# One-hot on Pool for 5120 columns, and half-block transfers, in a cross-entropy backward kernel

## The chip, the cores and the metric

One core of one Trainium2 chip. The metric is the device time of one launch in microseconds (us); lower is better. Unless a run is called slow, the times are of its fast runs. Each experiment ran beside runs of the kernel before on the same chip.

The problem is bound by memory traffic from the outset: 268.4 MB of float32 logits come in and 268.4 MB of result go out. All that a schedule can do is keep the 16 DMA engines busy from the first byte to the last.

## The reference, cut to what matters

```python
logits: (8, 1024, 8192) float32      labels: (8, 1024) int32
logits_max  = np.max(logits, axis=-1, keepdims=True)
exp_logits  = np.exp(logits - logits_max)
softmax     = exp_logits / np.sum(exp_logits, axis=-1, keepdims=True)
one_hot[batch_idx, seq_idx, labels] = 1.0
return (softmax - one_hot).astype(np.float32)
```

## The kernel before

The 8192 rows of 8192 columns are cut into 32 blocks of 256 rows. A partition holds two neighbouring rows of a block (j = 0, 1), so a block is 128 runs of 64 KB in HBM. Three block buffers in SBUF turn round. In what follows a "row" is one j, that is 128 rows of the problem, 4.19 MB; a block is two of them.

The mode strings have a letter for each block: r, each row is its own transfer (128 runs of 32 KB); w, the whole block is one transfer (128 runs of 64 KB); h, which the kernel before has in its table but doesn't use, two transfers, of the even and of the odd partitions (64 runs of 64 KB each).

```python
LOADS  = "rrrrrwwwwwwwwwwwwwwwwwwwwwrrrrrr"
STORES = "rrrrrrrrrrrrrrrrrrrrrrrrrrrrrrrr"
PIECES = {
    "r": [(every, slice(j, j + 1)) for j in range(G)],
    "h": [(slice(i, P, 2), rows) for i in range(2)],
    "w": [(every, rows)],
}
def load(b):            # issued by SP; waits for those stores of block b - 3 that touch the piece
    ...
def store(t):           # issued by ACT; a piece goes out when its last row is finished
    ...
for t in range(T):      # T = 64
    w = ACT  activation(Exp, bias=-max, accum_out=s)          # in place, 8192 columns
    w_sum = DVE reciprocal(r, s)
    if t + 1 < T:
        if (t + 1) % G == 0: load((t + 1) // G)
        w_max = row_max(t + 1)                                # DVE tensor_reduce
    if t > 0: store(t - 1)
    ACT  activation(Copy, scale=r)                            # 8192 columns
    DVE  scalar_tensor_tensor(x, iota == label, x - that)     # iota: int16 in PSUM
    ...                                                       # cut: last row in two parts
store(T - 1)
```

## Time and profile before

| | before |
|---|---|
| median | 1247.6 us |
| span of the profiled run | 1245.6 us |
| DVE busy | 1115.9 us |
| ACT busy | 919.0 us |
| DMA packets | 15,460 |
| 64 KB load packets, mean | 2421 ns |

The median is that of the timed runs, the next four rows are from the page of the profile, the last is from the packet records of the trace: one record for each contiguous run that a DMA engine moved, with its start and its duration. **Dry time** is how far the number of packets in flight fell short of 16 (one for each engine), integrated from the first data packet to the last and divided by 16. **Excess** is the time by which packets took longer than 2418 ns (64 KB) or 1213 ns (32 KB), which are their medians in this kernel, summed and divided by 16. The kernel before has 1.7 us of dry time and 2.3 us of excess: its engines are full, and its packets are as short as they get.

### The profile page before, as it was taken

The page shows a single profiled execution, that of the slowest core. Times are in us where ns is not written, and L with a number is a line of the kernel's source. Part 1 is how long each engine was busy: PE and PEld are TensorE (multiplying, and loading weights), DVE is VectorE, ACT ScalarE, POOL GpSimd, SP SyncE. Part 2 cuts the span into 40 slices and gives each one's busy share as a digit, 9 for nine tenths or more (in the row PEclk, how much of TensorE's full clock was granted, in tenths as well). Part 3 has the DMA queues.
Part 4 walks back from the last instruction along what each step waited for, and adds up shares of the span by engine and source line. Part 5 has one row for each costly group of instructions (what it writes and reads, how often), then busy time and mean ns, then how long its engine had stood idle before and what let it go on. Part 6 is the DMA issues. An engine that isn't in the chain of part 4 may idle for free.

```text
span 1245.6 us, 592 instructions
## 1 busy us (share of the span) xinstructions
PE 0.4 (0%) x2; PEld 0.3 (0%) x2; DVE 1115.9 (90%) x196; ACT 919.0 (74%) x194; POOL 7.4 (1%) x7
## 2 busy tenths in 40 slices
PE   0000000000000000000000000000000000000000
PEld 0000000000000000000000000000000000000000
DVE  4999997888988889888898888988889999999893
ACT  3888886678767787767867678777777788887772
POOL 2000000000000000000000000000000000000000
DMA  9999999999999999999999999999999999999998
GB/s 398 427 428 432 437 436 441 436 431 425 426 438 448 432 416 440 431 436 438 426 446 437 418 434 432 435 437 442 425 427 438 430 429 437 435 431 431 436 434 388
DMA packets 15460, 536.98 MB, mean 431 GB/s; under 512 B 1728, under 2 KB 1728, under 8 KB 1760
## 3 DMA queue, kind: packets, MB, share of 16 engines
q1 hardware_dynamic: 6240, 268.50, 50.0%
q10 hardware_dynamic: 9216, 268.44, 49.9%
q14 instruction: 4, 0.03, 0.0%
HBM read 268.50 MB, written 268.44 MB: 431 GB/s over the span
## 4 chain that ended last, share of the span: by engine, by line
DMA 60%; DVE 37%; ACT 1%; DVEq 0%; issue 0%; ACTq 0%; SPq 0%
DMA X<-in_logits_dram 32%; DMA out_dram<-X 28%; DVE m L68 19%; DVE X L68 18%; ACT X L68 1%; DVEq L56 0%; DVE r L68 0%; ACTq L68 0%; SPq L223 0%; SPq L56 0%
## 5 line engine op out<-in xcount | busy, mean ns | idle before, releaser
L68 DVE TENSOR_REDUCE m<-X 128x1 f32<-128x8192 f32 x64 | 555.2, 8674 | 108.5 <-DMA X<-in_logits_dram 108.5
L68 ACT ACTIVATE X<-X,m 128x8192 f32<-128x8192 f32 x64 | 455.8, 7122 | 190.2 <-DVE m L68 190.2
L68 DVE SCALAR_TENSOR_TENSOR X<-iota,lab,X 128x8192 f32<-128x8192 int16 (+1 forms) x65 | 559.6, 8611 | 4.1 <-ACT X L68 4.1
L68 ACT ACTIVATE X<-X,r 128x8192 f32<-128x8192 f32 (+1 forms) x65 | 456.0, 7016 | 115.4 <-DVE r L68 115.4
L68 ACT ACTIVATION_READ_ACCUMULATOR X<-X,m 128x1 f32 x64 | 12.0, 187 | 0.0
L68 DVE RECIPROCAL r<-s 128x1 f32<-128x1 f32 x64 | 9.8, 153 | 1.7 <-ACT X L68 1.7
L68 POOL IOTA X<- 128x8192 int16 x1 | 6.9, 6943 | 0.0
L68 DVE TENSOR_SCALAR iota<-X 128x4096 int32<-128x4096 int32 x1 | 4.4, 4428 | 0.1
L68 ACT ACT_TABLE_LOAD x1 | 1.3, 1283 | 0.9 <-SPq L56 0.9
L68 DVE COPY lab<-iota 128x64 f32<-128x64 f32 x1 | 0.2, 225 | 0.5 <-PE iota L68 0.5
L68 PE MATMUL iota<-ident,lab_f 32*128 32x32 f32 x2 | 0.4, 299 | 22.4 <-DVE lab_f L68 22.4
L68 DVE CAST lab_f<-lab_raw 32x256 f32<-32x256 int32 x1 | 0.4, 363 | 0.0
L68 PEld LDWEIGHTS iota<-ident,lab_f 32*128 32x128 f32 x2 | 0.3, 193 | 22.4 <-DVE lab_f L68 22.4
L68 POOL TENSOR_SCALAR_AFFINE_SELECT ident<-ident 32x32 f32<-32x32 f32 x1 | 0.2, 203 | 0.1
L68 POOL MEMSET ident<- 32x32 f32 x1 | 0.1, 115 | 0.5 <-SPq L56 0.5
L212 POOL MEMSET const-bfloat16-1.0<- 128x1 bf16 x1 | 0.1, 106 | 0.0
L212 POOL MEMSET const-uint8-127<- 128x1 uint8 x1 | 0.1, 106 | 0.0
L212 POOL MEMSET const-float32-0.0<- 128x1 f32 x1 | 0.1, 103 | 0.2 <-issue 0.2
L212 POOL MEMSET const-float32-1.0<- 128x1 f32 x1 | 0.1, 103 | 0.0
## 6 DMA issues: line engine op xcount, KB each, us to landing
out_dram<-X ACTq DMA_DIRECT2D x64, 4096.0 KB, 30.9
X<-in_logits_dram SPq DMA_DIRECT2D x22, 4096.0 KB, 27.5
X<-in_logits_dram SPq DMA_DIRECT2D x21, 33.2
lab_raw<-in_labels_dram SPq DMA_DIRECT2D x1, 64.0 KB, 12.3
```

Source lines behind the costliest of these rows:

```text
L68: instruction = getattr(engine, method)(**operands)
L212: nc = _bacc.Bacc("TRN2", target_bir_lowering=False, num_devices=1)
```

## The change

The intent: free ACT and shorten a row by letting idle Pool make most of the one-hot mask; and move 64 KB runs in both directions, in halves, so that the load of a slot's even partitions can start when the store of these has landed.

```diff
-LOADS = "rrrrrwwwwwwwwwwwwwwwwwwwwwrrrrrr"
-STORES = "rrrrrrrrrrrrrrrrrrrrrrrrrrrrrrrr"
+HOT = 5120
+CHUNK = 1280
+LOADS = "rrhhhhhhhhhhhhhhhhhhhhhhhhhhhrrr"
+STORES = "rrrrhhhhhhhhhhhhhhhhhhhhhhrrrrrr"
 ...            (labels, identity and iota are now made before the first row, in an X slot)
+        def row_hot(t):        # waits for w_used[t - 2], the reader of the same mask buffer
+            for k in range(0, HOT, CHUNK):
+                gpsimd.tensor_scalar(out=hot[:, t % 2, k : k + CHUNK], in0=chunk_iota,
+                                     scalar1=label(t) - k, op0=Alu.is_equal)     # int16 -> uint8
 ...
+        def row_finish(t, w_exp):
+            vector.reciprocal(r, s)
+            scalar.activation(x[:, rest], func=Copy, scale=r)                    # 3072 columns
+            vector.scalar_tensor_tensor(x[:, hot_cols], x[:, hot_cols] * r - hot[:, t % 2, :])
+            vector.scalar_tensor_tensor(x[:, rest], iota == label, x - that)     # as before
 ...
+        for b in range(B):
+            load(b); row_hot(2b); row_hot(2b + 1); row_max(2b); row_max(2b + 1)
+            store(2b - 1); row_exp(2b); row_finish(2b)
+            row_exp(2b + 1); store(2b); row_finish(2b + 1)
```

(Shortened: each call also carries its semaphores.)

More of the change, by code (lines that the diff above doesn't have):

```diff
@@ L36 @@
     B = T // G
+    REST = V - HOT
     lab_bp = labels.rearrange("a b -> (a b)").rearrange("(b q) -> b q", q=G * P)
@@ L45 @@
     X = const.tile([P, SLOTS, G, V], fp32)
-    lab_raw = const.tile([B, G * P], labels.dtype)
-    lab_f = const.tile([B, G, P], fp32)
-    ident = const.tile([B, B], fp32)
-    lab = const.tile([P, G, B], fp32)
+    lab = {k: const.tile([P, G, B], fp32, name=f"lab{k}") for k in range(0, HOT, CHUNK)}
     m, s, r = (const.tile([P, T], fp32, name=n) for n in ("m", "s", "r"))
-    iota = psum.tile([P, V], i16)
+    chunk_iota = const.tile([P, CHUNK], i16)
+    hot = const.tile([P, 2, HOT], mybir.dt.uint8)
+    iota = psum.tile([P, REST], i16)
     lab_ps = iota[:].bitcast(fp32)[:, :T].rearrange("p (j b) -> p j b", j=G)
-    with tc.tile_critical():
+    early = X[:, SLOTS - 1, 0, :]
+    lab_raw = early.bitcast(labels.dtype)[:B, : G * P]
+    at = G * P * mybir.dt.size(labels.dtype) // 4
+    lab_f = early[:B, at : at + G * P].rearrange("b (p j) -> b j p", j=G)
+    ident = early[:B, at + G * P : at + G * P + B]
+    made = X[:, SLOTS - 1, G - 1, :].bitcast(i16)[:, :REST]
+    with tc.tile_critical(no_gpsimd_drain=True):
         sem = tc.alloc_semaphore
-        got = [[sem(f"got{i}{q}") for q in range(2)] for i in range(SLOTS)]
-        put = [[sem(f"put{i}{q}") for q in range(2)] for i in range(SLOTS)]
+        got = [[sem(f"got{i}{j}") for j in range(G)] for i in range(SLOTS)]
+        put = [[sem(f"put{i}{j}") for j in range(G)] for i in range(SLOTS)]
         lab_got, dve, act, pe, pool = (sem(n) for n in ("lab_got", "dve", "act", "pe", "pool"))
@@ L74, in run @@
             return counter, count[counter.name]
+        w_raw = run(nc.scalar, [], lab_got, "dma_start", out=lab_raw, in_=lab_bp)
+        w = run(nc.gpsimd, [], pool, "memset", ap=ident, constant=0.0)
+        w_ident = run(
+            nc.gpsimd, [w], pool, "affine_select",
+            out=ident, in_=ident, compare_op=Alu.not_equal, fill=1.0,
+            base=0, pattern=[[-1, B]], channel_multiplier=1,
+        )
+        w_made = run(
+            nc.gpsimd, [], pool, "iota",
+            out=made, pattern=[[1, REST]], base=HOT, channel_multiplier=0,
+        )
+        w_chunk = run(
+            nc.gpsimd, [], pool, "iota",
+            out=chunk_iota[:], pattern=[[1, CHUNK]], base=0, channel_multiplier=0,
+        )
+        step = mybir.dt.size(labels.dtype) // 4
+        lab32 = lab_raw.bitcast(i32).rearrange("b (p j s) -> b j p s", j=G, s=step)
+        w_lab = run(nc.vector, [w_raw], dve, "tensor_copy", out=lab_f, in_=lab32[:, :, :, 0])
+        for j in range(G):
+            w = run(
+                nc.tensor, [w_ident, w_lab], pe, "transpose",
+                out=lab_ps[:, j, :], in_=lab_f[:, j, :], identity=ident,
+            )
+        for k in lab:
+            w_turned = run(
+                nc.vector, [w], dve, "tensor_scalar",
+                out=lab[k][:], in0=lab_ps, scalar1=float(k), scalar2=None, op0=Alu.subtract,
+            )
+        w_iota = run(
+            nc.vector, [w_turned, w_made], dve, "tensor_scalar",
+            out=iota[:].bitcast(i32), in0=made.bitcast(i32), scalar1=0, scalar2=None, op0=Alu.bitwise_or,
+        )
         every, rows = slice(0, P), slice(0, G)
@@ L87, in meets @@
             return all(x & y for x, y in zip(*sets))
-        loaded, stored, finished = {}, {}, []
-        last_made = []
-        def load(b, behind_first=lambda: None):
+        loaded, stored, finished = {}, {}, {}
+        def load(b):
             loaded[b] = []
-            before = stored.get(b - SLOTS, last_made if b == SLOTS - 1 else [])
+            before = stored.get(b - SLOTS, [((every, rows), w_iota)] if b == SLOTS - 1 else [])
             for q, piece in enumerate(PIECES[LOADS[b]]):
@@ L103, in load @@
                 loaded[b].append((piece, w))
-                if q == 0:
-                    behind_first()
         def store(t):
@@ L122, in row, with label @@
             return X[:, t // G % SLOTS, t % G, :]
+        def label(t, less=0):
+            return lab[less][:, t % G, t // G : t // G + 1]
+        w_max, w_sum, w_hot, w_used = {}, {}, {}, {}
+        def row_hot(t):
+            first = [w_chunk, w_turned] if t == 0 else [w_used[t - 2]] if t > 1 else []
+            for k in range(0, HOT, CHUNK):
+                w = run(
+                    nc.gpsimd, first if k == 0 else [], pool, "tensor_scalar",
+                    out=hot[:, t % 2, k : k + CHUNK], in0=chunk_iota[:],
+                    scalar1=label(t, k), scalar2=None, op0=Alu.is_equal,
+                )
+            w_hot[t] = w
         def row_max(t):
@@ L126, in row_max @@
             arrived = [w for piece, w in loaded[b] if meets(piece, (every, slice(j, j + 1)))]
-            return run(
+            w_max[t] = run(
                 nc.vector, arrived, dve, "tensor_reduce",
@@ L130, in row_max @@
             )
-        w_raw = []
-        load(0, lambda: w_raw.append(run(nc.sync, [], lab_got, "dma_start", out=lab_raw[:], in_=lab_bp)))
-        w_max = row_max(0)
-        w = run(nc.gpsimd, [], pool, "memset", ap=ident[:], constant=0.0)
-        w_ident = run(
-            nc.gpsimd, [w], pool, "affine_select",
-            out=ident[:], in_=ident[:], compare_op=Alu.not_equal, fill=1.0,
-            base=0, pattern=[[-1, B]], channel_multiplier=1,
-        )
-        made = X[:, SLOTS - 1, G - 1, :].bitcast(i16)[:, :V]
@@ L144 @@
-        w_made = run(
-            nc.gpsimd, [], pool, "iota", out=made, pattern=[[1, V]], base=0, channel_multiplier=0
-        )
-        step = mybir.dt.size(labels.dtype) // 4
-        lab32 = lab_raw[:].bitcast(i32).rearrange("b (p j s) -> b j p s", j=G, s=step)
-        w_lab = run(nc.vector, w_raw, dve, "tensor_copy", out=lab_f[:], in_=lab32[:, :, :, 0])
-        for j in range(G):
-            w = run(
-                nc.tensor, [w_ident, w_lab], pe, "transpose",
-                out=lab_ps[:, j, :], in_=lab_f[:, j, :], identity=ident[:],
-            )
@@ L155, with row_exp @@
-        w_turned = run(nc.vector, [w], dve, "tensor_copy", out=lab[:], in_=lab_ps)
-        w_iota = run(
-            nc.vector, [w_turned, w_made], dve, "tensor_scalar",
-            out=iota[:].bitcast(i32), in0=made.bitcast(i32), scalar1=0, scalar2=None, op0=Alu.bitwise_or,
-        )
-        last_made.append(((every, slice(G - 1, G)), w_iota))
-        for t in range(T):
+        def row_exp(t):
             x = row(t)
-            label = lab[:, t % G, t // G : t // G + 1]
-            w = run(
-                nc.scalar, [w_max], act, "activation",
+            return run(
+                nc.scalar, [w_max[t]], act, "activation",
@@ L168 @@
                 out=x, in_=x, func=Act.Exp, bias=m[:, t : t + 1], scale=1.0, accum_out=s[:, t : t + 1],
             )
-            w_sum = run(nc.vector, [w], dve, "reciprocal", out=r[:, t : t + 1], in_=s[:, t : t + 1])
-            if t + 1 < T:
-                if (t + 1) % G == 0:
-                    load((t + 1) // G)
-                w_max = row_max(t + 1)
+        def row_finish(t, w_exp):
+            x = row(t)
+            hot_cols, rest = slice(0, HOT), slice(HOT, V)
+            w_sum = run(nc.vector, [w_exp], dve, "reciprocal", out=r[:, t : t + 1], in_=s[:, t : t + 1])
+            w_rest = run(
+                nc.scalar, [w_sum], act, "activation",
+                out=x[:, rest], in_=x[:, rest], func=Act.Copy, bias=0.0, scale=r[:, t : t + 1],
+            )
+            w_used[t] = run(
+                nc.vector, [w_hot[t], w_sum], dve, "scalar_tensor_tensor",
+                out=x[:, hot_cols], in0=x[:, hot_cols], scalar=r[:, t : t + 1], in1=hot[:, t % 2, :],
+                op0=Alu.mult, op1=Alu.subtract,
+            )
+            finished[t] = run(
+                nc.vector, [w_rest], dve, "scalar_tensor_tensor",
+                out=x[:, rest], in0=iota[:], scalar=label(t), in1=x[:, rest],
+                op0=Alu.is_equal, op1=Alu.subtract, reverse1=True,
+            )
@@ L175 @@
+        for b in range(B):
+            load(b)
+            row_hot(b * G)
+            row_hot(b * G + 1)
+            t = b * G
+            row_max(t)
+            row_max(t + 1)
             if t > 0:
                 store(t - 1)
-            n = 1 if t + 1 < T else 2
-            cols = [slice(i * V // n, (i + 1) * V // n) for i in range(n)]
-            scaled = [
-                run(
-                    nc.scalar, [w_sum], act, "activation",
-                    out=x[:, c], in_=x[:, c], func=Act.Copy, bias=0.0, scale=r[:, t : t + 1],
-                )
-                for c in cols
-            ]
@@ L187 @@
-            for c, w in zip(cols, scaled):
-                w = run(
-                    nc.vector, [w], dve, "scalar_tensor_tensor",
-                    out=x[:, c], in0=iota[:, c], scalar=label, in1=x[:, c],
-                    op0=Alu.is_equal, op1=Alu.subtract, reverse1=True,
-                )
-            finished.append(w)
+            w = row_exp(t)
+            row_finish(t, w)
+            w = row_exp(t + 1)
+            store(t)
+            row_finish(t + 1, w)
         store(T - 1)
@@ L196 @@
             for _, w in stored[b]:
-                nc.scalar.wait_ge(*w)
+                nc.sync.wait_ge(*w)
 _INS = ['logits', 'labels']
```

## The prediction

> **What bounds the kernel now.** I read the page first: engine shares, the slices, the queues.
>
> ```profile
> PE 0.4 (0%) x2; PEld 0.3 (0%) x2; DVE 1115.9 (90%) x196; ACT 919.0 (74%) x194; POOL 7.4 (1%) x7
> ...
> DMA  9999999999999999999999999999999999999998
> ...
> DMA packets 15460, 536.98 MB, mean 431 GB/s; under 512 B 1728, under 2 KB 1728, under 8 KB 1760
> ...
> q1 hardware_dynamic: 6240, 268.50, 50.0%
> q10 hardware_dynamic: 9216, 268.44, 49.9%
> ```
>
> The reader is to see that DVE is 90% busy and yet not the bound: the DMA row is 9 in all slices but one. 268.4 MB in and 268.4 MB out are the least the problem allows, and no part of the change moves fewer bytes. Then the chain of waits in order of time, for what a block costs:
>
> ```profile
> 906.93 27.44 DMA out_dram<-X
> 934.39 33.30 DMA X<-in_logits_dram
> 967.71 8.69 DVE m L68
> 976.40 8.66 DVE X L68
> ```
>
> From one such store to the next it is some 77.4 us, for two blocks of 256 rows: 38.7 us a block. A block is 8.39 MB in and 8.39 MB out; 16.78 MB in 38.7 us is 433.5 GB/s. So the chain, though it passes through 17.4 us of DVE, goes at the pace of the queues: its transfers stretch to fill the time. The windows of 20 us say the same, DMA share 0.95 to 1.07 from 20 us to 1240 us. The packet records of the trace settle it: 16 packets (one for each DMA engine) are in flight at nearly every instant of the 1242 us from the first data packet to the last. There is next to no DMA idle time to recover; before and after those 1242 us lie 3.5 us of span, and the timed median is 2.0 us above the span (1247.63 against 1245.6).
>
> The durations for the working come from the groups, with shapes kept apart:
>
> ```profile
> L68 DVE TENSOR_REDUCE m<-X 128x1 f32<-128x8192 f32 x64 | 555.2, 8674 | 108.5 <-DMA X<-in_logits_dram 108.5
> L68 DVE SCALAR_TENSOR_TENSOR X<-iota,lab,X 128x8192 f32<-128x8192 int16 x63 | 550.7, 8742 | 0.0
> L68 ACT ACTIVATE X<-X,m 128x8192 f32<-128x8192 f32 x64 | 455.8, 7122 | 190.2 <-DVE m L68 190.2
> ...
> L68 DVE SCALAR_TENSOR_TENSOR X<-iota,lab,X 128x4096 f32<-128x4096 int16 x2 | 8.9, 4480 | 4.1 <-ACT X L68 4.1
> L68 ACT ACTIVATE X<-X,r 128x4096 f32<-128x4096 f32 x2 | 7.3, 3700 | 1.8 <-DVE r L68 1.8
> L68 POOL IOTA X<- 128x8192 int16 x1 | 6.9, 6943 | 0.0
> ```
>
> The reader is to see two sizes of the same operation, which give a slope and a fixed part, and that DVE waits 108.5 us in all for loads: compute waits for DMA, not the reverse.
>
> **What the Trainium skill says.** (1) "DMA: Bandwidth & Descriptors", section "Where 436 GB/s comes from": 16 ports of 32 B at 850 MHz give 435.2 GB/s. The trace agrees: 433.5 in the middle. At that rate 536.98 MB take 1234 us, so no schedule of these bytes can be 2% faster (under 1222.7). (2) Same page, "Queues, rings and completion order": each DMA engine takes turns between queues packet by packet. So 64 KB load packets against 32 KB store packets favour loads, and equal packets share evenly; the trace's 8 MB loads (33.3 us) beside 4 MB stores (27.4 us) fit. (3) "SBUF — State Buffer", "Who interferes with whom": a DVE instruction with two SBUF inputs and a GpSimd instruction that reads SBUF exclude each other, and the later one waits for the whole of the earlier. The kernel before cannot show it: its iota lies in PSUM, and Pool is silent after 8 us. (4) "GPSIMD Engine Reference", section 7: a compare body took 2.03 cycles an element, 1.03 when unrolled. No row before has a Pool compare; IOTA's 6943 ns for 8192 is 1.02 cycles at 1.2 GHz.
>
> **The change, part by part.**
>
> Transfers. The packet records give 1213 ns for 32 KB and 2418 ns for 64 KB: 8 ns saved where one large packet replaces two. Before: 11,008 small (8192 stores, 2816 loads) and 2,688 large. After: loads are 5 blocks by rows (1,280 small) and 27 in halves (3,456 large); stores are 10 by rows (2,560 small) and 22 in halves (2,816 large). So 3,584 pairs merge: 3,584 x 8 ns / 16 engines = **1.8 us less**. Half transfers also double the semaphore packets of a block move, 9 ns each: nothing.
>
> ACT. The scaling falls from 8192 to 3072 columns. 8192 take 7.12 us and 4096 take 3.70: 0.835 ns a column and 0.28 fixed, so 2.85 us. ACT loses 64 x 4.27 = 273 us of busy time. It was not the bound, so this is worth nothing directly.
>
> DVE. The last step becomes 5120 and 3072 columns. Slope (8.74 - 4.48)/4096 = 1.04 ns, fixed 0.22: 5.55 + 3.41 = 8.96 us, and consecutive ones overlap by 0.1. The busy time stays near 64 x (8.67 + 8.96 + 0.15) = 1138 us.
>
> Schedule of one block (two rows) after its load, with starts on DVE: two maxima 0 to 17.2; exp of the first row meanwhile on ACT (8.7 to 16.0); reciprocal 17.3; compared part 17.5 to 23.0; rest 23.0 to 26.3 (ACT's Copy ends at 20.4). ACT's second exp runs 20.4 to 27.7, so DVE idles 1.4 us. Second reciprocal 27.8, compared part 28.0 to 33.5, rest to 36.8. So **36.8 us a block** against 38.7 of DMA: DMA still sets the pace, by 1.9 us. Before, DVE needed 2 x 17.44 = 34.9 us a block, so the new order is tighter.
>
> Pool. Four compares of 1280 a row. At 1.03 to 2.03 cycles an element, 1.2 GHz and an assumed 0.1 us of start, one is 1.2 to 2.3 us and a row 4.8 to 9.1 us (an estimate from the GPSIMD page). A row's compares may begin only when the buffer's reader two rows earlier has ended, that is at 23.0 in the block, and the second compared part wants to start at 28.0: 5.0 us later. With fast compares Pool is just done; with slow ones DVE waits for the compare in flight, at most 2.3 us. The other row's compares (from 33.5) fall beside the maxima and harm nobody. I put the block at 37.5.
>
> Start and end. Label work leaves the path behind the first maximum and runs before the first row lands (13.4 us): neutral. A loss: a half load needs both row stores of its slot. Walking the start at 433 GB/s, row stores go out near 42, 51, 79, 88 us; the queues run dry for perhaps 1 us near 79, when the load of block 3 waits for the store of row 1 to land, and for up to 2.5 us near 196, when block 4 (first stored in halves) finishes as both queues empty. At the end, row stores again: with four rows outstanding at the last load, the last two come 19 and 28 us later, just in time; up to 3 us may be lost. I take **2 us of new DMA idle time** in all, out of a possible 0 to 6.
>
> Sum: 1247.6 - 1.8 + 2.0 = 1247.8; the kernel's strings of modes look chosen by trial, which makes me lean to less idle time: **1246.5 us**.
>
> **Rivals.** (a) Compute takes over: the block exceeds 38.7 us. First row after 13.4 us, then 32 blocks, then about 15 us for the last store: 28.4 + 32 x C. C = 38.0 gives 1244, so it begins to bind there; C = 38.8 (the worst single wait) gives 1270; C = 40 gives 1308. For it: DVE at 90%, the two SBUF inputs, Pool's compares starting right ahead of the contended step. Against it: only one compare should be in the way, and short chunks look meant for that. If Pool held the ports for all four compares in a row, C would near 41 and the time 1340. (b) Transfers over 64 alternate partitions go slower than over 128: nothing in the profile before speaks of such a transfer, since it has none; at 5% less the time would be 1305. Even and odd partitions spread over the same places, so I give it little. (c) The relief of ACT and earlier loads shorten the time: against it, the DMA row is full everywhere, so at most a microsecond or two at the ends. (d) The new waits at the changes of mode cost more than I walked through, say 8 us: 1254.
>
> **Range and chances.** Floor: no new idle and a little better packing, 1243. Likely: 1245 to 1250. (d) and mild (a) reach 1262. So 1242 to 1260 should hold 8 times in 10. Faster by 2% is barred by bytes over rate: 0.01. Slower by 2% (over 1272.6) needs rival (a) in its bad form or (b): 0.08. Within: 0.91.
>
> **What would show it.** Right: DMA slices still 9 throughout, near 433 GB/s; fewer packets (about 12,200 in all); ACT near 646 us, DVE near 1140 us plus contention, Pool 310 to 580 us; the chain still mostly DMA; 64 KB packets still 2418 ns. Wrong: DMA slices of 8 and DVE at 9 to 10 throughout with the compared step well over 5.55 us would mean rival (a); long packets at full DMA share, rival (b); single low slices near 80 and 196 us or at the end, rival (d). The weakest steps are the Pool compare's duration and who yields when it meets DVE.

## The result

The changed kernel takes **1267.9 us** (median of 4 runs, 1265.5 to 1268.4) against 1247.6 us (1247.3 to 1248.1). The ratio is 1.0158, 95% interval 1.0141 to 1.0176: slower by 1.6%, within 2%, but outside the range I had given. (A ratio here is the mean time of one kernel's fast runs over that of the other's fast runs of the same rounds, so not quite the ratio of the medians.)

The page of the changed kernel: engine shares, the DMA row and the rate in 40 slices, the packet count, and three groups (busy time and mean of one | idle time before, and for what).

```profile
PE 0.4 (0%) x2; PEld 0.3 (0%) x2; DVE 1186.3 (94%) x262; ACT 642.5 (51%) x193; POOL 1076.4 (85%) x264
...
DMA  9999998999999999999999999999999999999996
GB/s 400 415 423 430 434 429 359 431 429 432 440 431 423 440 440 442 431 431 428 431 429 429 429 431 434 431 442 436 434 432 431 429 432 424 430 431 437 433 417 284
DMA packets 12216, 537.01 MB, mean 425 GB/s; under 512 B 2064, under 2 KB 2064, under 8 KB 2096
...
L80 POOL TENSOR_SCALAR hot<-chunk_iota,lab 128x1280 uint8<-128x1280 int16 x256 | 1072.1, 4196 | 154.7 <-DVE X L80 153.3
...
L80 DVE TENSOR_REDUCE m<-X 128x1 f32<-128x8192 f32 x64 | 552.9, 8679 | 23.2 <-DMA X<-in_logits_dram 23.2
L80 DVE SCALAR_TENSOR_TENSOR X<-X,r,hot 128x5120 f32<-128x5120 f32 x64 | 411.0, 6422 | 2.3
```

Read it against the lines of before in the prediction. ACT fell by 276 us, as worked out, and it bought nothing. DVE rose by 70 us: its 5120-column step takes 6.42 us on average. Pool's compare takes 4.2 us for 1280 columns. And the DMA row, full before, has two holes: slice 7 (190 to 221 us) at 359 GB/s and the last slice at 284.

The time line of one block in the middle (start, duration, engine, what; in brackets the idle time before and its releaser) shows the meeting of DVE and Pool:

```profile
573.89 5.55 DVE L80 SCALAR_TENSOR_TENSOR X<-X,r,hot 128x5120 f32<-128x5120 f32 x1
...
579.54 32.82 POOL L80 TENSOR_SCALAR hot<-chunk_iota,lab 128x1280 uint8<-128x1280 int16 x8 [6.45 <-DVE X L80]
...
584.09 7.37 DVE L80 SCALAR_TENSOR_TENSOR X<-X,r,hot 128x5120 f32<-128x5120 f32 x1
591.38 3.40 DVE L80 SCALAR_TENSOR_TENSOR X<-iota,lab,X 128x3072 f32<-128x3072 int16 x1
```

The first row's step takes 5.55 us while Pool stands still. It frees Pool's buffer, Pool starts eight compares, and the second row's step, 4.5 us later, takes 7.37 us: 1.82 us more. If eight compares share the 32.82 us with one DVE step of 5.55 us, a compare takes 3.4 us, and the second one would end 6.8 us after 579.54, at 586.4; 584.09 + 1.82 is 585.9. The two agree to half a microsecond: the step waits for about the rest of the compare in flight, then goes ahead of the next one.

The end of the changed kernel, the four last stores that ACT issues:

```profile
1202.33 0.34 ACTq L80 DMA_DIRECT2D out_dram<-X  x1
...
1214.34 0.34 ACTq L80 DMA_DIRECT2D out_dram<-X  x1
...
1240.51 0.34 ACTq L80 DMA_DIRECT2D out_dram<-X  x1
...
1250.70 0.34 ACTq L80 DMA_DIRECT2D out_dram<-X  x1
```

All loads have landed by then. 26 us pass between the second and third of these stores; a row takes some 10 us to move alone (4.19 MB at 433 GB/s), so the queue runs out.

**Where the 17 us went, by the packet records.** From the first data packet to the last the changed kernel takes 1259.3 us against 1242.1. Dry time rose from 1.7 to 13.6 us (3.9 us from 170 to 215 us, 8.8 us from 1220 us on). Excess rose from 2.3 to 8.6 us, nearly all of it in 64 KB loads, whose mean is 2453 ns against 2421. Merged packets gave back 1.8 us. 11.9 + 6.3 - 1.8 = 16.4 us; packets overlap a little less, which is the rest. This is book-keeping: idle engines and long packets must add up to the time, and it names no cause. The question is whether the compute made the transfers late, or the transfers themselves are worse.

### The profile page after: what moved, and what is told of

Its sections match the earlier page's. It is cut to its first block, busy times and chain, and to the rows that moved or that the text cites. A ratio compares the mean times of both kernels' runs of the same rounds, so it can differ in the third digit from the quotient of the medians.

```text
span 1263.7 us, 1041 instructions
## 1 busy us (share of the span) xinstructions
PE 0.4 (0%) x2; PEld 0.3 (0%) x2; DVE 1186.3 (94%) x262; ACT 642.5 (51%) x193; POOL 1076.4 (85%) x264
## 2 busy tenths in 40 slices
DMA packets 12216, 537.01 MB, mean 425 GB/s; under 512 B 2064, under 2 KB 2064, under 8 KB 2096
## 4 chain that ended last, share of the span: by engine, by line
DMA 39%; DVE 28%; ACT 12%; POOL 10%; issue 10%; ACTq 0%; SPq 0%; DVEq 0%
DMA out_dram<-X 22%; DMA X<-in_logits_dram 17%; DVE m L80 15%; DVE X L80 12%; ACT X L80 12%; POOL hot L80 10%; DVE r L80 0%; ACTq L80 0%; SPq L80 0%; DVEq L79 0%; SPq L261 0%; SPq L68 0%
## 5 line engine op out<-in xcount | busy, mean ns | idle before, releaser
L80 POOL TENSOR_SCALAR hot<-chunk_iota,lab 128x1280 uint8<-128x1280 int16 x256 | 1072.1, 4196 | 154.7 <-DVE X L80 153.3
L80 DVE TENSOR_REDUCE m<-X 128x1 f32<-128x8192 f32 x64 | 552.9, 8679 | 23.2 <-DMA X<-in_logits_dram 23.2
L80 DVE SCALAR_TENSOR_TENSOR X<-X,r,hot 128x5120 f32<-128x5120 f32 x64 | 411.0, 6422 | 2.3
L80 DVE SCALAR_TENSOR_TENSOR X<-iota,lab,X 128x3072 f32<-128x3072 int16 x64 | 218.1, 3408 | 0.0
L80 ACT ACTIVATE X<-X,r 128x3072 f32<-128x3072 f32 x64 | 182.8, 2857 | 56.8 <-DVE r L80 56.8
L80 POOL IOTA X<- 128x3072 int16 x1 | 2.7, 2677 | 0.0
```

The lines of the kernel that those rows point to most:

```text
L80: instruction = getattr(engine, method)(**operands)
```

## The experiments

Theory A: the compute. DVE's step meets Pool's compares, a block takes 38.0 to 38.2 us in place of 36.3, and so the queues go dry at both ends. Theory B: the order, both maxima ahead of the first finish, which makes the last stores late. Theory C: the transfers in halves.

### Strings and compute taken apart (e1, e2)

```diff
 e1: the changed kernel
-LOADS = "rrhhhhhhhhhhhhhhhhhhhhhhhhhhhrrr"        +LOADS = "rrrrrwwwwwwwwwwwwwwwwwwwwwrrrrrr"
-STORES = "rrrrhhhhhhhhhhhhhhhhhhhhhhrrrrrr"       +STORES = "rrrrrrrrrrrrrrrrrrrrrrrrrrrrrrrr"
 e2: the kernel before, with the opposite edit
```

> The changed kernel with the two mode strings of the kernel before (row and whole-block loads, row stores); the compute is the changed one. Theory A (compute has become the pace at both ends: DVE's compared step meets Pool's compares, 38.0 to 38.2 us a block instead of 36.3): the block stays at 38.0 to 38.2 us, the queues still run dry near the end, time 1260 to 1268 us. Theory C (the half transfers cost it: the dry spell near 190 us and the slower 64 KB load packets): both go away, time 1248 to 1256 us.

> The kernel before with the mode strings of the changed kernel; the compute is the old one. Theory A: no loss, 1245 to 1250 us, 64 KB packets at 2418 ns. Theory C: 1255 to 1265 us, with 64 KB load packets averaging above 2440 ns and a dry spell of some us where the stores change to halves.

e1: **1249.0 us**, ratio to before 1.0003 (0.9988 to 1.0018), correct. e2: **1281.4 us**, ratio 1.0264 (1.0244 to 1.0284). Theory C wins outright, and for e2 by more than it asked: by the ratios the strings cost 2.6% (33 us) with the old compute and 1.6% (19 us) with the new. The whole new compute, contention and order included, costs under 1 us. The page of e1:

```profile
PE 0.4 (0%) x2; PEld 0.3 (0%) x2; DVE 1183.2 (95%) x262; ACT 642.3 (51%) x193; POOL 1153.2 (92%) x264
...
DMA  9999999999999999999999999999999999999998
...
L80 DVE TENSOR_REDUCE m<-X 128x1 f32<-128x8192 f32 x64 | 552.6, 8672 | 10.4 <-DMA X<-in_logits_dram 10.4
L80 DVE SCALAR_TENSOR_TENSOR X<-X,r,hot 128x5120 f32<-128x5120 f32 x64 | 409.7, 6401 | 2.3
```

The step takes as long as ever (6.40 us), and the DMA row is full again. The telling figure is in the first group: the maxima wait 10.4 us in all for loads, 23.2 us in the changed kernel. (On the first two rows it is 3.7 us in e1 and 6.0 us in the changed kernel; the rest comes later.) At 38.1 us a block, compute has 0.6 us a block to spare against the 38.7 us of transfers, so one reading is that compute can't catch up on late loads, and the last stores are late for it. e3, below, speaks against this as the whole cause. The order alone (Theory B) costs nothing either: e1 has the same order and only 2.4 us of dry time.

### Pool's compares taken out, and the ports taken apart (e3, e4, e5, e12)

```diff
 e3: the changed kernel
         def row_hot(t):
+            if t > 1:
+                w_hot[t] = w_hot[t - 2]
+                return
 e4: the changed kernel; fake is a uint8 tile in PSUM, set to 0 once
-                ... in1=hot[:, t % 2, :],
+                ... in1=fake[:],
 e5: e3 with the old LOADS and STORES
 e12: the changed kernel
-CHUNK = 1280
+CHUNK = 640
```

> The changed kernel, but Pool compares only for rows 0 and 1 and later rows use those masks (wrong result on purpose). Everything else stays. Theory A: the 5120-column step falls from a mean of 6.42 to 5.55 us, the block to 36.3 us, the DMA idle time near the end shrinks, time 1248 to 1256 us. Theory C: block shorter too, but time 1260 or more, since the transfers are the same. Theory B (the order: both maxima ahead of the first finish, so that the last stores come late): time stays above 1258 us with a dry spell of 6 us or more at the end.

> The changed kernel with Pool's compares as they are, but DVE's 5120-column step reads its mask from a constant tile in PSUM (wrong result on purpose), so that it has one SBUF input. Theory A, in the form that the two exclude each other over SBUF inputs: the step takes 5.55 us though Pool is as busy, Pool's compares take 3.4 to 3.5 us each and never stand still for the step, and the time equals that of the run with Pool silent within 2 us. If Pool's work slows DVE in another way: the step stays near 6.4 us and the time near 1266 us.

> The changed kernel with both suspects taken out: Pool compares only for rows 0 and 1 (wrong result on purpose) and the two mode strings are those of the kernel before. With the run that had only the strings at 1249.0 us: if the meeting of DVE and Pool costs nothing while transfers are good, 1246 to 1249 us. If it costs by itself what it seems to cost beside the half transfers (some 6 us), 1241 to 1244 us. DMA share full to the end in either case.

> The changed kernel with Pool's compares cut to 640 columns, eight a row. Theory A (DVE's 5120-column step waits for the compare in flight, 1.6 to 1.8 us of a 3.4 us compare in the second row of a block): a compare takes near 1.8 us, the wait is at most that, the mean of the step falls from 6.42 to between 5.6 and 6.1 us, time 1260 to 1266 us. If DVE must wait for a whole row of compares or for Pool's queue: the mean stays at 6.4 us or rises, time 1266 us or more.

e3: 1262.3 us (1258.3 to 1264.4), ratio 1.0099. e4: 1256.9 us in the median of its three fast runs (1256.8 to 1260.8), ratio 1.0077, and one run of 1399.9 that counts as slow (it has no trace; what it was is open). e5: 1248.5 us, ratio 1.0007. e12: 1262.6 us (1260.9 to 1275.0), ratio 1.0139 (1.0091 to 1.0187). Two groups of e4, two of e12, and of e3 the DMA row, the rate and the maxima:

```profile
L81 POOL TENSOR_SCALAR hot<-chunk_iota,lab 128x1280 uint8<-128x1280 int16 x256 | 897.5, 3517 | 316.7 <-DVE X L81 312.6
...
L81 DVE SCALAR_TENSOR_TENSOR X<-X,r,fake 128x5120 f32<-128x5120 f32 x64 | 355.1, 5548 | 2.3
```

```profile
L80 POOL TENSOR_SCALAR hot<-chunk_iota,lab 128x640 uint8<-128x640 int16 x512 | 1227.1, 2416 | 5.2 <-DVE lab L80 5.2
...
L80 DVE SCALAR_TENSOR_TENSOR X<-X,r,hot 128x5120 f32<-128x5120 f32 x64 | 366.7, 5730 | 19.5 <-POOL hot L80 17.8
```

```profile
DMA  9999999999999999999999999999999999999996
GB/s 401 431 408 432 433 446 407 434 438 430 432 424 440 434 432 428 436 432 428 434 432 428 432 432 432 432 432 432 430 428 430 430 432 425 429 423 433 428 408 290
...
L80 DVE TENSOR_REDUCE m<-X 128x1 f32<-128x8192 f32 x64 | 553.0, 8680 | 68.3 <-DMA X<-in_logits_dram 68.3
```

With the mask in PSUM, DVE's step has one SBUF input and takes 5.55 us, though Pool makes all 256 compares; and a compare takes 3.52 us in place of 4.20. So both had been waiting for each other, and over SBUF inputs. (I had expected the time of e4 within 2 us of e3's; its fast runs are 5 us below.) With compares of half the size the step's mean falls from 6.42 to 5.73 us, as it should if the wait is for one compare in flight. The mean of 2.42 us for 640 columns includes compares that stood still for DVE; in the median one takes 1.88 us, as expected, and one of 1280 columns 3.51 us in the changed kernel: 2.56 ns a column and a fixed 0.24 us. With the waits Pool is busy for 98% of the span, and DVE waits 17.8 us for masks. The contention is shown; so is its price. By the ratios (1.0158 against 1.0099 and 1.0077) it is some 7 to 10 us with the new strings, and with the old nothing that can be measured (1.0003 with it, 1.0007 without). In these runs it hurts only beside the new strings.

e3 missed the range of Theory A (1248 to 1256 us); those of C (1260 or more) and of B (above 1258 us, 6 us or more dry at the end) hold. Its compute is ahead of the loads (the maxima wait 68.3 us), and what then binds are the transfers: 11.0 us of excess and 10.3 us of dry time. Of the dry time 9.4 us lie after 1220 us, as in the changed kernel (8.8; 4.7 in e4), though here compute had slack, and though the spell near 190 us is gone (in e4 too, with the same strings). By the packet records the last load landed at 1215.8 us in e3 and at 1215.2 us in the changed kernel, against 1200.4 us in e1. So late loads go with a dry end also where compute is not short of time. e1 clears the order alone; whether the order together with these strings costs anything at the end no run separates.

### Loads or stores (e6, e7, e9, e10)

```diff
 e6: the kernel before     +LOADS = "rrhhhhhhhhhhhhhhhhhhhhhhhhhhhrrr"
 e7: the kernel before     +STORES = "rrrrhhhhhhhhhhhhhhhhhhhhhhrrrrrr"
 e9: the changed kernel    +STORES = "rrrrrrrrrrrrrrrrrrrrrrrrrrrrrrrr"
 e10: the changed kernel   +LOADS = "rrrrrwwwwwwwwwwwwwwwwwwwwwrrrrrr"
```

> The kernel before with the changed LOADS string alone; stores stay row by row. Theory C1 (half loads are slow in themselves: 64 KB load packets of a mean of 2530 ns against 2421 for whole-block loads): mean above 2480 ns, time 1262 us or more. Theory C2 (half stores cost it, by coming in lumps of two rows): packets near 2425 ns, time 1246 to 1252 us.

> The kernel before with the changed STORES string alone; loads stay by rows and whole blocks. Theory C1: load packets at 2420 to 2430 ns, time 1245 to 1250 us. Theory C2: time 1262 us or more, with dry spells.

> The changed kernel with row stores throughout (the old STORES string); loads stay in halves. Theory L (the loss comes from stores that are handed over two rows at a time, so that loads run for some us with no store beside them, slowly, and the queues run dry at the changes of mode): the dry spell near 190 us goes, 64 KB load packets average near 2430 ns, time 1249 to 1257 us. If half loads by themselves are to blame: time stays at 1262 us or more.

> The changed kernel with the old LOADS string (whole-block loads in the middle) and the changed stores in halves. Theory L: a whole-block load must wait for both halves of the store, so it starts when the store queue is empty and runs alone: as in the kernel before with half stores alone (1366 us), 1330 to 1390 us, dry spells of about 3 us a block and 64 KB load packets above 2600 ns. If half stores only hurt in the old row order: under 1275 us.

With e1, e2 and the two kernels these complete the eight combinations (medians in us):

| loads, stores | old compute | new compute |
|---|---|---|
| old, old | 1247.6 | 1249.0 (e1) |
| halves, old | 1255.7 (e6) | 1256.2 (e9) |
| old, halves | 1366.2 (e7) | 1332.5 (e10) |
| halves, halves | 1281.4 (e2) | 1267.9 (changed) |

Half loads alone cost 7 to 8 us whatever the compute; their 64 KB packets average 2435 ns in e6 and 2450 ns in e9. e9's time is inside Theory L's range, and the spell near 190 us is gone. e10's time is too, but its dry spells are nearer 1 us a block than the 3 I expected. Half stores are bad with any loads, and ruinous beside whole-block loads: there a load of 8 MB waits for both halves of the store, and each block begins with empty queues. The critical chain of e7, in order of time (start, duration, what), for one turn:

```profile
557.45 35.49 DMA out_dram<-X
592.94 0.02 issue
592.96 34.53 DMA X<-in_logits_dram
627.49 0.02 issue
627.52 8.69 DVE m L68
636.20 8.66 DVE X L68
...
645.41 35.54 DMA out_dram<-X
```

In the kernel before the same turn, from a store on this chain to the next, took 77.4 us; here it takes 88.0 us (557.45 to the next store at 645.41), again for two blocks. Theory C1, that half loads are slow in themselves, had said 2420 to 2430 ns and 1245 to 1250 us for e7: as the whole cause it falls, since e7's loads are ordinary whole blocks and yet average 2663 ns. C2, lumps of two rows, is right for e7 and says too little for e6, whose stores go by rows and which still loses 8 us.

### Address or partition (e8)

```diff
 e8: e2 with
-  out=X[ps, b % SLOTS, js, :], in_=x_b[b, ps, js, :]
+  out=X[ps, b % SLOTS, js, :], in_=x_b[b, slice(q * 64, q * 64 + 64) if LOADS[b] == 'h' else ps, js, :]
```

> The kernel before with both changed strings, but a half load reads 64 neighbouring 64 KB runs of HBM in place of every second one, and still writes even or odd partitions (wrong result on purpose). If the slow packets come from the step of 128 KB between runs in HBM: mean back to 2420 to 2430 ns, time 1248 to 1258 us. If they come from writing alternate partitions, or from the half shape: mean near 2530 ns and time near 1281 us, as with both strings and the true addresses.

1282.0 us (1279.6 to 1284.2), load packets at 2534 ns, as in e2 (1281.4 us, 2530 ns). The step between the runs that the loads read in HBM is not the cause. (The result was wrong, yet passed the comparison: exchanged rows differ only in softmax values, which are small beside the ones of the one-hot.)

### Slow when alone? (e11)

```diff
 e11: the kernel before    +LOADS = "wwwrrwwwwwwwwwwwwwwwwwwwwwrrrrrr"
```

> The kernel before, but the first three loads are whole blocks, 64 KB packets, where it has rows, 32 KB packets; in the first 45 us or more no store is in flight. The kernel before ran its 32 KB packets at 1217 to 1220 ns in that stretch (2435 per 64 KB). If 64 KB loads are slow when they are alone and back to back: well above 2600 ns in that stretch, as after the dry spells (3000 to 3700 ns). If they are only slow just after the queues were empty: the first wave slow, the rest 2420 to 2440 ns. The time itself, some us longer since the first maximum waits for 8 MB, is not the point.

A single run of 1254.7 us, state unknown; only its packets matter. In the first 57 us, with no store in flight, the first 16 packets of 64 KB averaged 3115 ns, those after them 2418 to 2432, but for 17 at 20 to 23 us, between two transfers (2504 to 2753), and the 16 that began at 58.7 to 59.5 us (2928 on average), after ACT had issued the first store at 56.9 us. So 64 KB loads are not slow for being alone. In the traces of the changed kernel, e2 and e7 the long packets stand in bunches of one or two waves of 16, as many as there are engines: after a dry spell (16 packets from 203.3 us in the changed kernel: 3145 ns) and beside it where a store starts next to loads that had run alone (the next 16: 3421 ns; ACT had issued the store at 203.6 us). Each such start costs a wave of packets 0.5 to 1.2 us. That is what I see, not a mechanism.

### The ends, the match of the modes, and a slow way of running (e13 to e17)

```diff
 e13: the kernel before    +LOADS = "rrrrrhhhhhhhhhhhhhhhhhhhhhrrrrrr"
 e14: the changed kernel   +LOADS = "rrrrrhhhhhhhhhhhhhhhhhhhhhrrrrrr"
                           +STORES = "rrrrrrrrrrrrrrrrrrrrrrrrrrrrrrrr"
 e15: the changed kernel   +LOADS = "rrrrrrrhhhhhhhhhhhhhhhhhhhhhhrrr"     (STORES as changed)
 e16: e15 with Pool for two rows, as in e3
 e17: e16 with w for each h, in both strings
```

> The kernel before, half loads exactly where it had whole-block loads (blocks 5 to 25), row stores. If the half shape itself costs: 1253 to 1257 us, as with the changed LOADS string (1255.7). If the loss came from fewer row loads at the two ends: 1246 to 1250 us.

> The changed kernel, half loads only in blocks 5 to 25, row stores. If the half shape costs: 1254 to 1258 us, as with half loads in blocks 2 to 28 (1256.2). If the ends cost: 1247 to 1251 us, as with the old strings (1249.0).

> The changed kernel with its half stores in blocks 4 to 25, and half loads only in blocks 7 to 28, so that each half load waits for a half store of the same partitions and each row load for a row store. If the change of mode costs (the dry spell near 190 us, the slow load packets after it, and compute never catching up): the dry spell goes, time 1250 to 1259 us. If not: 1263 to 1268 us as before.

> As e15 with Pool comparing only rows 0 and 1 (wrong result on purpose). If the late compute and the mode change are one loss seen twice, equal to e15 within 2 us; if two, 4 to 8 us below e15. A time below 1246 us would show that halves with matched modes and an unhindered DVE can beat the kernel before by their larger packets.

> As the run with matched modes and Pool for two rows (wrong result on purpose), but whole blocks (one transfer over 128 partitions, the same 64 KB packets) wherever that had halves, for loads and for stores. If the slow packets belong to 64 KB in both queues: loads still above 2700 ns, time above 1350 us. If they belong to the halves: load packets 2420 to 2480 ns apart from the first after a dry spell; the time may still be 1260 to 1330 us, because a whole load must wait for a whole store and the queues run dry for some us in each block.

e13: 1250.6 us, ratio 1.0022 (1.0007 to 1.0037). e14: 1253.8 us, ratio 1.0054 (1.0037 to 1.0071). Both lie between the two forecasts: of the 8 us that half loads cost with the old compute, 5 go with the six blocks towards the two ends (2 to 4 and 26 to 28) and 3 with the 21 in the middle; with the new compute the 7 us split into 2 and 5. (Differences of medians: 1255.7 - 1250.6 and 1250.6 - 1247.6; 1256.2 - 1253.8 and 1253.8 - 1249.0.)

e15: 1257.3 us, ratio 1.0076 (1.0036 to 1.0117), runs from 1251.8 to 1263.7. When each half load waits for a half store of the same partitions and not for two row stores, the dry spell near 190 us is gone, and so is about half of the loss, as forecast. But e15 also has five half loads fewer at the start, and half loads towards the ends cost 5 us in e6 against e13; and the spell is gone in e3 and e4 with the strings unchanged; so the match of the modes is not shown to be the cause. The rate in 40 slices of its profiled run, which was its fastest:

```profile
GB/s 405 419 435 433 432 431 432 427 434 430 436 434 428 428 434 426 430 436 436 436 436 436 436 436 434 434 432 428 432 434 430 436 432 434 428 425 434 432 433 357
```

e16, which should have been faster still, took **1424 to 1468 us** (ratio of its fast runs 1.1445). The rate of its profiled run, which counts as slow by the rule of 1.5% above the fastest of the same kernel (the two runs that count as fast took 1423.9 and 1432.9):

```profile
GB/s 402 428 430 432 439 436 397 376 368 349 363 347 341 320 366 343 331 336 359 334 338 336 359 334 334 340 366 340 331 329 372 340 336 329 386 366 434 429 430 320
```

It starts and ends like e15. From the first half store on it falls to 320 to 370 GB/s and stays there until the row modes return. Load packets of 64 KB average 2966 ns and stores 2637, not in bunches but throughout, with 14 to 16 packets in flight. Its 138.7 us of excess and 86.5 us of dry time add up to the whole of it. e17, with whole blocks in the same places, took 1278.3 and 1290.3 us in its fast runs (the other two, 1299.4 and 1314.1, count as slow); its loads average 2549 ns, between the two forecasts, in bunches at the start of a transfer, with long stretches at 2418. So in this pair the lasting slow way goes with the halves, and the bunches come with either shape. The halves are not enough for it: e15 has the same strings, and e3 the same compute, and neither shows it. (The slow run of e4, 1399.9 us, may be the same way; without a trace that is open.) Neither forecast for e16 held; both had assumed that halves at best cost nothing more.

**Dry time and excess of the profiled runs** together account for the time (us; idle engines and long packets must add up to it, so this says where the time is, not why):

| run | span | dry | excess |
|---|---|---|---|
| before | 1245.6 | 1.7 | 2.3 |
| changed | 1263.7 | 13.6 | 8.6 |
| e1 | 1247.4 | 2.4 | 3.2 |
| e5 | 1247.0 | 2.7 | 2.5 |
| e3 | 1262.6 | 10.3 | 11.0 |
| e4 | 1259.1 | 5.6 | 12.2 |
| e15 | 1250.1 | 3.9 | 5.1 |
| e6 | 1252.5 | 5.1 | 6.0 |
| e9 | 1256.2 | 5.4 | 9.1 |
| e2 | 1276.7 | 8.9 | 27.1 |
| e17 | 1288.5 | 11.8 | 35.8 |
| e10 | 1328.2 | 31.2 | 55.4 |
| e7 | 1365.0 | 74.8 | 49.0 |
| e16 | 1466.7 | 86.5 | 138.7 |

No version beat the kernel before. The best of those with the changed compute and a right result is e1, its compute with the old strings, which equals it.

## Why the prediction was wrong

**What bounds the kernel, and the floor**: right. The DMA engines did, and no run came below 1247 us.

**The step that failed** is the transfers' part of the sum, "- 1.8 + 2.0": both of its terms. In the profiled runs the packets brought + 6.3 - 1.8 and the idle time + 11.9.

**"3,584 pairs merge ... 1.8 us less. Half transfers also double the semaphore packets ...: nothing"**: the merge is real (12,216 packets, as counted), but I took the packet's duration as a constant of its size. It depends on what the queues are doing: 64 KB loads averaged 2453 ns here, 2421 before and 2966 in e16. Excess grew by 6.3 us where I had taken 1.8 off. I had named this as rival (b), half transfers slower than whole ones, and given it little, for a reason that no row of the profile before could show, since none had such a transfer. (b) is half right: half loads alone cost 7 to 8 us (e6, e9), but e7's whole-block loads lengthen too.

**"I take 2 us of new DMA idle time in all, out of a possible 0 to 6"**: too small; it rose by 11.9 us. The place near 196 us was right, and the size of that spell (2.5 at most; 3.9 measured) nearly; in part this is luck, since e3 and e4 have the same strings and no such spell. The end was not: up to 3 us foreseen, 8.8 found. What goes with the dry end is the lateness of the last load: it landed at 1215.2 us, 15 us later than with the old strings and the same compute (e1, 1200.4), and in e1 only 1.7 us at the end are dry. My first reading, that compute without slack carries the delay to the end, fits the changed kernel, whose compute waits for no load after 1062 us, but it is not shown to be the cause: e3's compute has slack, and its end is as dry.

**Rival (d), the waits at the changes of mode**: the sign I had named for it, single low slices near 196 us and at the end, is what the page shows; I had put it at 8 us (1254 us).

**"36.8 us a block ... I put the block at 37.5"**: mis-sized. It is 38.0 to 38.2. (The 38.8 that I gave for the worst single wait doesn't follow from my own numbers: 36.8 + 2.3 is 39.1.) The schedule was right to a few tenths (the compared step starts 10.2 us after the first row's; I had 10.5). Pool's compare was not: 3.5 us of its own time against 1.2 to 2.3. The wait it causes, 1.6 to 1.8 us, stayed within my 2.3, since the step waits for the rest of one compare and no more. So the slack was 0.6 us a block and not 1.2.

**Rival (a), compute takes over**: half right. 28.4 + 32 x C gives 1244 to 1251 for C = 38.0 to 38.2; e1, whose chain of waits is mostly compute, took 1249.0. Compute does draw level with the transfers, at no measurable loss beside the old strings; beside the new ones its meeting with Pool costs the 7 to 10 us above.

**ACT's relief is worth nothing directly; DVE and GpSimd exclude each other over SBUF inputs**: both right (e4 for the second).

**What stays open.** Why packets lengthen: at the start of a transfer, and lastingly in e16. The step in HBM is excluded (e8), being alone is excluded (e11), the size of 64 KB in both queues is not enough for the lasting form (e17). Why loads land late and the end runs dry in e3, whose compute has slack, is open as well.

## What to carry to other kernels

Where the DMA engines are full, the duration of a packet is a result, not a constant: measure a new transfer shape alone in the running kernel before counting on its larger packets. Keep both queues supplied in small, steady pieces, and let a load wait only for the store of the same piece; handing over two rows at once empties a queue (e7: about 3 us a block), and each restart costs. Before relieving an engine that isn't the bound, look at the slack of the engine that takes on the work: here it went from 3.8 us a block to 0.6.

## What the Trainium skill lacked or had wrong

- "GPSIMD Engine Reference", section 7, gives 2.03 cycles an element for a body of compare and select, 1.03 when unrolled by two, in a list for hand-written kernels; I took it for the compare instruction. Here is_equal of int16 against a scalar of each partition, to uint8, took 3.52 us for 1280 columns (e4, where nothing held it up) and 1.88 us for 640 (e12, in the median): 2.56 ns a column, which is 3.1 cycles at the page's 1.2 GHz, and a fixed 0.24 us.
- "SBUF — State Buffer", "Who interferes with whom", is right on who excludes whom (e4: 5.55 us in place of 6.42, and 3.52 in place of 4.20). It says that the later one waits for the earlier instruction, not who goes next when Pool has more queued: here DVE did, after 1.6 to 1.8 us.
- "DMA: Bandwidth & Descriptors", "Queues, rings and completion order", says that an engine drains a packet of typically 9 to 17 descriptors from one queue before it turns to the other. The records show turns after single 64 KB runs: near 228 to 240 us in the changed kernel 16 stores, 16 loads, 16 stores, 16 loads in turn.
- No page has the lengthening of large packets: 2418 ns in the median for 64 KB, waves of 2930 to 3630 ns on average after a dry spell or at the start of a store beside loads (changed kernel, e7, e11), and 2966 ns on average throughout e16, with half transfers in both directions.
- "DMA: Bandwidth & Descriptors", "Rules for kernel authors", says of two transfers to disjoint partition halves not to bother, since they serialize. For even and odd partitions that holds beside row stores: the halves lose 3 us (e13). Beside half stores it does not: half loads are 65 to 85 us faster than whole-block loads (changed kernel against e10, e2 against e7), since each can start when its own half of the store has landed.
